# Attention by couples of heads or maps: fp32 scores on 64-row tiles, A's values on 64-column tiles, nothing split

## The chip, the cores and the metric

The kernel runs on one core of one Trainium2 chip. The metric is the device time of one execution in microseconds, the median over several runs. The core has five engines with queues of their own: TensorE (PE), VectorE (DVE), ScalarE (ACT), GpSimd (POOL) and SyncE (SP), which here issues all DMAs. A queue runs in order; an engine whose next instruction waits does nothing else.

## The reference

One encoder layer, applied to two request groups (prompt, sample) of 1024 tokens and 1024 channels with the same weights. A normalised and modulated input `h` is projected once; two attention branches read it, and their gated outputs are projected, merged and added to the input.

```python
mod = einsum('bd,de->be', silu(c), w_ada) + b_ada;  shift, scale, gate = split(mod, 3)
h = rms_norm(x, norm_g) * (1 + scale) + shift
qa, ka, va, za, qb, kb, vb, zb, ga, gb = split(h @ w_in)
# A: 8 query heads, 2 key/value heads, head size 64; RMSNorm and axial rotation of q and k
oa = softmax(qa @ ka.T / 8) @ va * silu(za)
# B: 4 heads, two softmax maps of size 64 per head, values of 128
pd = softmax(q0 @ k0.T / 8) - lam * softmax(q1 @ k1.T / 8)
ob = rms_norm(pd @ vb, subln_g) * (1 - lam_init) * silu(zb)
merged = sigmoid(ga) * (oa @ w_proj_a) + sigmoid(gb) * (ob @ w_proj_b)
return x + gate * (merged @ w_out)
```

## The kernel before

All data is fp32. Where precision is needed at the speed of single-pass products (type `fp32r`), an operand is split into a rounded part and the rest, and the products of the parts are added up in PSUM. The kernel does this for the weights and `h` (three products for one), for the queries and keys of all scores, and for A's values. Only B's values are plain fp32 products (`WHOLE`, L810).

For each group the program runs a head (keys and values of A, the first half of A's queries), then six phases of attention, then the projections. A phase weaves three streams: attention steps (`attention`), the projections for the next phase (`qa_gen`, `qkb_gen`, `vb_gen`, products at L497) and the gate paths (`z_gen`, products at L679). The weaving by shares (`ATT_W` and the like) and a priority for attention steps set where instructions stand; a scheduler puts them in each engine's order when the program is built, and nothing is moved at run time.

- `pairs_T` turns queries and keys by a PE transpose (L548). Each head's 64 rows are then written twice over 128 partitions: rounded on one half (L550, ACT), the rest on the other (L551, DVE). `swapped` makes a second copy of a piece of 256 queries with the halves exchanged, by two or four DMAs (tile `sw`).
- `scores` handles one head or map and one query tile of 128: four products over 128 partitions (L709 with the tile `q`, L710 with `sw`) fill one of two score tiles `s` in PSUM, 128 x 1024. DVE takes the maximum (L711), ACT the exponential with its sum (L712), which frees the tile.
- `flip` combines B's two maps (L744), transposes in blocks of 32 x 32 (L745, DVE) and regroups by four DMAs into a tile `q`, two query tiles making a unit of 256.
- `a_values`: for each of four pieces the turned probabilities are split (L758, ACT; L759, DVE), and 16 products of 256 columns (L770, L771) go into the one accumulator `a`. Since the values are split too, rows 0-63 and 64-127 of `a` are two parts of one head, added at L786 and L787.
- `b_values`: eight fp32 products of 256 columns (L810), no split.

A unit is one head (A) or one head of two maps (B) with 256 queries: per group 32 units in A and 16 in B. PSUM has two tiles `s`, three banks `f` for the projections and one bank `a`.

Of the kernel before, what the change touches and what calls it, by code (L numbers as in the profile page):

```python
# [64 lines left out]
BEHIND = 1.4  # L65
AHEAD = 100
PV_LAG = 2

WHOLE = (True, True)
# [21 lines left out]
def kernel(ctx: ExitStack, tc: tile.TileContext, t: dict):  # L91
# [8 lines left out]
    qpool = ent(tc.tile_pool(name="qpool", bufs=2))  # L100
    tpool = ent(tc.tile_pool(name="tpool", bufs=2))
# [403 lines left out]
    def rms(ps, nh, e):  # L505
# [3 lines left out]
        nc.scalar.activation(raw, ps, AF.Copy)  # L509
# [31 lines left out]
    def pairs_T(x3, even, odd):  # L541


        nb = x3.shape[1] // 2
        ps = gbank()[:, : nb * P].rearrange("p (b n) -> p b n", b=nb)
        x = x3.rearrange("p (b two) d -> p b (two d)", two=2)
        for b in range(nb):
            nc.tensor.transpose(ps[:, b, :], x[:, b, :], ident)  # L548
        for dst, hi, lo in ((even, LO, HI), (odd, HI, LO)):
            nc.scalar.activation(dst[hi], ps[hi], AF.Copy)  # L550
            nc.vector.tensor_tensor(out=dst[lo], in0=ps[hi], in1=dst[hi].bitcast(F32), op=ALU.subtract)  # L551
# [15 lines left out]
    def swapped(u):  # L567

        qs = u["q"]
        sw = mtile("sw", [P, 2, 256], F32R)[:, : len(qs)]  # L570
        sl = slice(u["pr"] * 256, u["pr"] * 256 + 256)
        for m, q in enumerate(qs):
            for a, b in ((LO, HI), (HI, LO)):
                dma(sw[a, m].bitcast(F32), q[b, sl].bitcast(F32))
        return sw


    made = {}

# [3 lines left out]
    def kva_gen(ht, out):  # L583
        w = kva_w.pop()[0] if kva_w else load_w(w_cols(w_in, (C_KA, 256)))
        k = v2(utile())
        va = utile().rearrange("p (n k d) -> p n k d", n=NTT, k=2)
        out["ka"], out["va"] = k, va

        def front(tt, ps):
            e = by_turns(tt)  # L590
            x3, s3 = rms(ps[:, :128], 2, e)
            vp = ps[:, 128:256].rearrange("p (k d) -> p k d", k=2)
            vt = va[:, tt]
            nc.scalar.activation(vt[:, :, 0:64], vp, AF.Copy)
            nc.vector.tensor_tensor(out=vt[:, :, 64:128], in0=vp, in1=vt[:, :, 0:64].bitcast(F32), op=ALU.subtract)
            e.tensor_tensor(out=x3, in0=x3, in1=gka.unsqueeze(1).to_broadcast([P, 2, HD]), op=ALU.mult)
            rope(x3, s3, out["cosA"][:, tt], out["sinA"][:, tt], 16, e)
            return x3

        def back(tt, x3):  # L600
            sl = slice(tt * P, (tt + 1) * P)
            pairs_T(x3, k[:, 0:1, sl], k[:, 1:2, sl])
# [3 lines left out]
    def qa_gen(st, half):  # L606
        w = load_w(w_cols(w_in, (C_QA + half * 256, 256)))
        qs = [v2(utile()), v2(utile())]
# [3 lines left out]
        def front(tt, ps):  # L612
            e = by_turns(tt)
            x3, s3 = rms(ps, 4, e)
# [4 lines left out]
        def back(tt, x3):  # L619
            sl = slice(tt * P, (tt + 1) * P)  # L620
            pairs_T(x3, qs[0][:, :, sl], qs[1][:, :, sl])
            made[id(qs)] = tt + 1
# [3 lines left out]
    def qkb_gen(ht, out, h):  # L626
        w = load_w(w_cols(w_in, (C_QB + h * P, P), (C_KB + h * P, P)))
        qk = out[h] = (v2(utile()), v2(utile()))
# [9 lines left out]
        def back(tt, x3):  # L638
            sl = slice(tt * P, (tt + 1) * P)
            pairs_T(x3, qk[0][:, :, sl], qk[1][:, :, sl])  # L640
            made[id(qk)] = tt + 1
# [3 lines left out]
    def vb_gen(ht, out, pr):  # L645
        w = load_w(w_cols(w_in, (C_VB + pr * 256, 256)))
        if WHOLE[pr]:
            v = utile().bitcast(F32).rearrange("p (n h e) -> p n h e", n=NTT, h=2)
            out[2 * pr], out[2 * pr + 1] = v[:, :, 0], v[:, :, 1]
        else:  # L650
            vs = [utile().rearrange("p (n s e) -> p n s e", n=NTT, s=2) for _ in range(2)]
            out[2 * pr], out[2 * pr + 1] = vs
        for tt in range(NTT):
            ps = yield from proj_tt(ht, w, tt)
            if WHOLE[pr]:
                nc.scalar.activation(v[:, tt].rearrange("p h e -> p (h e)"), ps, AF.Copy)
                yield 1
                continue
            for i in range(2):
                vp = ps[:, i * P : (i + 1) * P]  # L660
                nc.scalar.activation(vs[i][:, tt, 0, :], vp, AF.Copy)
                nc.vector.tensor_tensor(
                    out=vs[i][:, tt, 1, :], in0=vp, in1=vs[i][:, tt, 0, :].bitcast(F32), op=ALU.subtract
                )
# [38 lines left out]
    def softmax_unit(q, sw, k, pt, su):  # L703

        m = tiny.tile([P, 1], F32, tag="m", name=nm("m"))
        s = sbank()
        for n in range(2):
            sl = slice(n * 512, (n + 1) * 512)
            nc.tensor.matmul(s[:, sl], q, k[:, sl], start=True, stop=False)  # L709
            nc.tensor.matmul(s[:, sl], sw, k[:, sl], start=False, stop=True)  # L710
        nc.vector.tensor_reduce(out=m, in_=s, axis=AX.X, op=ALU.max, negate=True)  # L711
        nc.scalar.activation(  # L712
            pt.rearrange("p (j c a) -> p j c a", j=4, c=8), s.rearrange("p (c a j) -> p j c a", c=8, j=4),
            AF.Exp, bias=m, accum_out=su,
        )

    def scores(u, i):

        nm_ = len(u["q"])
        t, m = i // nm_, i % nm_  # L720
        qt = u["pr"] * 2 + t
        if "sw" not in u:
            u["sw"] = swapped(u)
        pt = ptile()
        su = u["su"][:, qt : qt + 1] if m == 0 else tiny.tile([P, 1], F32, tag="su", name=nm("su"))
        softmax_unit(u["q"][m][:, qt * P : (qt + 1) * P], u["sw"][:, m, t * P : (t + 1) * P], u["k"][m], pt, su)
        if m == 0:
            u[t] = [pt]
        else:
            f = tiny.tile([P, 1], F32, tag="r", name=nm("r"))  # L730
            nc.vector.reciprocal(f, su)
            nc.gpsimd.tensor_scalar(
                out=f, in0=f, scalar1=u["su"][:, qt : qt + 1], scalar2=nlam, op0=ALU.mult, op1=ALU.mult
            )
            u[t] += [pt, f]
        return t if m == nm_ - 1 else None

    def flip(u, t):


        pt = u[t][0]
        if len(u[t]) > 1:
            _, p1, f = u[t]
            nc.vector.scalar_tensor_tensor(out=pt, in0=p1, scalar=f, in1=pt, op0=ALU.mult, op1=ALU.add)  # L744
        nc.vector.transpose(pt, pt)  # L745
        if t == 0:
            u["pT"] = pair(F32R)
        dst = u["pT"].bitcast(F32).rearrange("p (i t f) -> p i t f", i=4, t=2)
        for i in range(4):
            dma(dst[:, i, t], pt[i * 32 : i * 32 + 32])  # L750

    def pT_pieces(u):

        pT = u["pT"].rearrange("p (q c b) -> p c q b", q=8, c=8)
        for cc in range(4):
            tl = pT[:, cc * 2 : cc * 2 + 2]
            th = tpool.tile([P, 2, 8, 32], F32R, tag="hi", name=nm("hi"), bufs=3)
            nc.scalar.activation(th, tl.bitcast(F32), AF.Copy)  # L758
            nc.vector.tensor_tensor(out=tl, in0=tl.bitcast(F32), in1=th.bitcast(F32), op=ALU.subtract)  # L759
            yield cc, th, tl  # L760

    def a_values(u):
        acc = ps_a.tile([P, 512], F32, tag="a", name=nm("a"))[:, :256]
        ready = []

        def pv(cc, th, tl):
            for c in range(2):
                k = cc * 2 + c
                lt = u["v"](k)
                nc.tensor.matmul(acc, lt, th[:, c, :], start=(k == 0), stop=False)  # L770
                nc.tensor.matmul(acc, lt, tl[:, c, :], start=False, stop=(k == 7))  # L771

        for piece in pT_pieces(u):
            ready.append(piece)
            if len(ready) > PV_LAG:
                pv(*ready.pop(0))
            yield 1
        while len(ready) > 1:
            pv(*ready.pop(0))
            yield 1  # L780
        pv(*ready.pop())
        tmp = mtile("at", [P, 256], bufs=1)
        o = mtile("oo", [P, 256])
        j = u["j"]
        a, b = (slice(0, 64), slice(64, 128)) if j % 2 == 0 else (slice(64, 128), slice(0, 64))
        nc.scalar.activation(tmp[a], acc[b], AF.Copy)  # L786
        nc.vector.tensor_tensor(  # L787
            out=query_order(o[a]), in0=piece_order(acc[a]), in1=piece_order(tmp[a]), op=ALU.add
        )
        pr = u["pr"]  # L790
        dma(u["od"][pr // 2][a, (pr % 2) * 256 : (pr % 2 + 1) * 256], o[a])
        yield 1

    def b_values(u):
        acc = ps_a.tile([P, 512], F32, tag="a", name=nm("a"))[:, :256]
        ready = []
        def pv(cc, th, tl):
            for c in range(2):
                k = cc * 2 + c
                for s, rt in ((0, th), (0, tl), (1, th)):  # L800
                    nc.tensor.matmul(
                        acc, u["v"][:, k, s, :], rt[:, c, :],
                        start=(k == 0 and s == 0 and rt is th), stop=(k == 7 and s == 1),
                    )

        if WHOLE[u["h"] // 2]:
            pT = u["pT"].bitcast(F32).rearrange("p (q c b) -> p c q b", q=8, c=8)
            yield 1
            for k in range(NCH):
                nc.tensor.matmul(acc, u["v"][:, k], pT[:, k], start=(k == 0), stop=(k == 7))  # L810
                if k % 2:
                    yield 1
        else:
            for piece in pT_pieces(u):
                ready.append(piece)
                if len(ready) > PV_LAG:
# [365 lines left out]
```

## Time and profile before

| | |
|---|---|
| median of 3 runs | 1984.13 us (1981.57 to 1989.72) |
| span of the profiled execution, the only time that the page gives of it | 1985.5 us |
| PE busy / weight loads busy | 1908.6 us / 1627.8 us |
| DVE, ACT, POOL busy | 1330.8, 1009.9, 758.1 us |
| mean granted TensorE clock | 0.982 |
| records of products, each with a weight load | 10466 |

The page gives busy times per engine, the span in 40 slices, the chain of work that ended last, and groups of instructions by source line. A row of a group reads: line, engine, operation, tile written <- tiles read, shape, count | busy us, mean ns of one | idle time of the engine just before them and what ended it. PEld are PE's weight loads, which have rows of their own. In a timeline a row is start, length (both us), engine, line, operation and count. An fp32 product leaves two records, an `fp32r` product one. Records of products overlap at their ends, so their rate is read from the starts.

### The profile page before, as it was taken

The page shows a single profiled execution, that of the slowest core. Times are in us where ns is not written, and L with a number is a line of the kernel's source. Part 1 is how long each engine was busy: PE and PEld are TensorE (multiplying, and loading weights), DVE is VectorE, ACT ScalarE, POOL GpSimd, SP SyncE. Part 2 cuts the span into 40 slices and gives each one's busy share as a digit, 9 for nine tenths or more (in the row PEclk, how much of TensorE's full clock was granted, in tenths as well). Part 3 has the DMA queues.
Part 4 walks back from the last instruction along what each step waited for, and adds up shares of the span by engine and source line. Part 5 has one row for each costly group of instructions (what it writes and reads, how often), then busy time and mean ns, then how long its engine had stood idle before and what let it go on. Part 6 is the DMA issues. An engine that isn't in the chain of part 4 may idle for free.

```text
span 1985.5 us, 30670 instructions
## 1 busy us (share of the span) xinstructions
PE 1908.6 (96%) x10466; PEld 1627.8 (82%) x10466; DVE 1330.8 (67%) x1906; ACT 1009.9 (51%) x1939; POOL 758.1 (38%) x1008
## 2 busy tenths in 40 slices
PE   8889999999999998999999899999999999999999
PEld 3878888888878994778888787888887888877887
DVE  4558877777877577547465877677788845665641
ACT  4435655665654444754323565556655534566310
POOL 2374612453446252221235464134445626422110
PEclk9899999999999999999999999999999999999999
DMA  8124556555553345865641455565654333567532
GB/s 310 33 80 126 155 152 169 152 166 154 133 153 102 101 120 173 257 227 167 222 149 35 140 144 145 149 164 144 184 137 137 106 97 99 156 212 245 174 101 75
DMA packets 269531, 295.11 MB, mean 149 GB/s; under 512 B 35776, under 2 KB 218176, under 8 KB 269376
## 3 DMA queue, kind: packets, MB, share of 16 engines
q1 hardware_dynamic: 269376, 293.15, 49.7%
q8 instruction: 84, 1.38, 0.3%
q14 instruction: 71, 0.58, 0.1%
HBM read 133.59 MB, written 42.01 MB: 88 GB/s over the span
## 4 chain that ended last, share of the span: by engine, by line
PE 68%; DMA 8%; DVE 8%; ACT 5%; SPq 4%; issue 3%; POOL 3%; ACTq 0%; POOLq 0%; DVEq 0%
PE f L497 16%; PE f L679 16%; PE f L950 6%; PE f L979 5%; PE s L709 4%; PE a L810 4%; PE s L710 4%; PE s L979 4%; DMA q<-p 3%; SPq L750 3%; PE s L950 2%; DVE q L759 2%; PE a L771 2%; PE a L770 2%; DVE m L711 2%
## 5 line engine op out<-in xcount | busy, mean ns | idle before, releaser
L679 PE MATMUL f<-u,w 128*128 128x512 f32 x2232 | 582.3, 398 | 0.1
L497 PE MATMUL f<-w,u 128*128 128x256 f32 x3456 | 487.0, 286 | 2.2 <-ACT ev L685 1.4
L497 PEld LDWEIGHTS f<-w,u 128*128 128x128 f32 x3456 | 459.5, 192 | 22.4 <-ACT ev L685 1.8
L679 PEld LDWEIGHTS f<-u,w 128*128 128x128 f32 x2232 | 408.8, 190 | 77.3 <-POOL w L181 0.8
L181 POOL TENSOR_TENSOR w<-st,w 128x512 fp32r<-128x512 f32 x168 | 230.3, 1390 | 439.9 <-ACT w L179 375.1
L712 ACT ACTIVATE p<-s,m 128x1024 f32<-128x1024 f32 x256 | 284.4, 1111 | 206.3 <-DVE m L711 111.3
L711 DVE TENSOR_REDUCE m<-s 128x1 f32<-128x1024 f32 x256 | 310.0, 1216 | 51.3 <-PE s L710 48.7
L745 DVE STREAM_TRANSPOSE p<-p 128x1024 f32<-128x1024 f32 x192 | 238.2, 1241 | 99.2 <-ACT p L712 86.5
L759 DVE TENSOR_TENSOR q<-q,hi 128x512 fp32r<-128x512 f32 x256 | 198.3, 792 | 60.6 <-ACT hi L758 58.6
L515 POOL TENSOR_TENSOR rs<-ss,nhalf 128x4 f32<-128x4 f32 (+1 forms) x112 | 112.8, 1007 | 322.8 <-DVE ss L514 284.0
L758 ACT ACTIVATE hi<-q 128x512 fp32r<-128x512 f32 x256 | 153.8, 625 | 104.1 <-DMA q<-p 55.4
L710 PE MATMUL s<-u,sw 128*128 128x512 f32 x512 | 206.7, 404 | 0.0
L179 ACT ACTIVATE w<-st 128x512 fp32r<-128x512 f32 x196 | 113.9, 625 | 97.2 <-DMA st<-in_w_in_dram 46.0
L950 PE MATMUL f<-u,w 128*128 128x512 f32 x552 | 133.4, 395 | 5.1 <-ACT ev L685 4.4
L770 PE MATMUL a<-hi,u 128*128 128x256 f32 x512 | 132.5, 285 | 2.1 <-DVE oo L787 2.1
L771 PE MATMUL a<-q,u 128*128 128x256 f32 x512 | 129.8, 286 | 1.2 <-DVE q L759 1.2
L810 PE MATMUL a<-q,u 128*128 128x256 f32 x512 | 128.3, 390 | 1.9 <-DVE oo L826 1.5
L950 PEld LDWEIGHTS f<-u,w 128*128 128x128 f32 x552 | 103.9, 190 | 27.2 <-ACT ev L685 4.7
L709 PE MATMUL s<-u 128*128 128x512 f32 x256 | 110.9, 433 | 15.1 <-ACT p L712 15.1
L810 PEld LDWEIGHTS a<-q,u 128*128 128x128 f32 x512 | 97.8, 196 | 17.5 <-DVE oo L826 1.6
L709 PE MATMUL s<-u,u 128*128 128x512 f32 x256 | 103.6, 405 | 8.3 <-ACT p L712 7.7
L710 PEld LDWEIGHTS s<-u,sw 128*128 128x128 f32 x512 | 98.4, 192 | 15.5
(175 smaller groups left out, 2562.1 us busy)
## 6 DMA issues: line engine op xcount, KB each, us to landing
q<-p SPq DMA_DIRECT2D x768, 128.0 KB, 2.6
st<-in_w_in_dram SPq DMA_DIRECT2D x132, 256.0 KB, 3.0
zd<-ev SPq DMA_DIRECT2D x96, 256.0 KB, 2.2
sw<-u SPq DMA_DIRECT2D x256, 64.0 KB, 2.1
p<-zd SPq DMA_DIRECT2D x64, 256.0 KB, 3.2
u<-in_w_ada_dram SPq DMA_DIRECT2D x8, 1024.0 KB, 10.4
st<-in_w_in_dram SPq DMA_DIRECT2D x64, 128.0 KB, 2.7
st<-in_w_out_dram SPq DMA_DIRECT2D x32, 256.0 KB, 2.9
```

The source lines that it names most:

```text
L181: e.tensor_tensor(out=wl, in0=st, in1=wh.bitcast(F32), op=ALU.subtract)
L497: nc.tensor.matmul(ps, lt[c][:, sl], w[:, c, wi, :], start=(k == 0), stop=(k == 23))
L679: nc.tensor.matmul(ps, w[:, c, wi, e * P : (e + 1) * P], rt[c], start=(k == 0), stop=(k == 23),)
L709: nc.tensor.matmul(s[:, sl], q, k[:, sl], start=True, stop=False)
L710: nc.tensor.matmul(s[:, sl], sw, k[:, sl], start=False, stop=True)
L711: nc.vector.tensor_reduce(out=m, in_=s, axis=AX.X, op=ALU.max, negate=True)
L712: nc.scalar.activation(pt.rearrange("p (j c a) -> p j c a", j=4, c=8), s.rearrange("p (c a j) -> p j c a", c=8, j=4), AF.Exp, bias=m, accu ...
L745: nc.vector.transpose(pt, pt)
L759: nc.vector.tensor_tensor(out=tl, in0=tl.bitcast(F32), in1=th.bitcast(F32), op=ALU.subtract)
L810: nc.tensor.matmul(acc, u["v"][:, k], pT[:, k], start=(k == 0), stop=(k == 7))
L950: nc.tensor.matmul(ps, w[:, c, wi, d * P : (d + 1) * P], o[:, oi, :], start=(k == 0), stop=(k == 11))
L979: nc.tensor.matmul(ps, w[:, c, wi, e * P : (e + 1) * P], m[:, mi, :], start=(k == 0), stop=(k == 23))
```

## The change

Two heads of A that share a place in their key/value groups (j and j + 4), or the two maps of a B head, form a couple. One transpose puts the first in partitions 0-63 and the second in 64-127, and one ACT copy writes them, unsplit, in fp32 (`turned` in place of `pairs_T`). The columns of A's query weights are loaded in an order that makes such couples. `swapped` and its DMAs are gone, and so are the splits of the probabilities and of A's values.

`scores` now handles a couple and a query tile: four fp32 products of 512 columns, alternating between partitions 64-127 and 0-63, into both tiles `s` at once. Each contracts over 64 partitions and so uses a tile of 64 rows of the array. `a_values` makes 16 fp32 products of 256 columns, alternating between two column halves of the array: the first head's values end in rows 0-63 of `a`, the second's in 64-127, and one ACT copy takes both out. Nothing is added up. `together` binds the products of one group so that nothing stands between them; the first score product of a couple also waits for both exponentials of the couple before. A has 16 units per group (couples with 256 queries), B 16 as before. The pool of regrouped tiles grows from two to three, the pool of split pieces goes. The steps and their shares in the weaving are rewritten for the new count (`PAIRS`).

```diff
+PAIRS = (1.3, 0.3)
+TOP = 100000
-PV_LAG = 2
-WHOLE = (True, True)
...
-    qpool = ent(tc.tile_pool(name="qpool", bufs=2))
-    tpool = ent(tc.tile_pool(name="tpool", bufs=2))
+    qpool = ent(tc.tile_pool(name="qpool", bufs=3))
...
-        for dst, hi, lo in ((even, LO, HI), (odd, HI, LO)):
-            nc.scalar.activation(dst[hi], ps[hi], AF.Copy)
-            nc.vector.tensor_tensor(out=dst[lo], in0=ps[hi], in1=dst[hi].bitcast(F32), op=ALU.subtract)
+        nc.scalar.activation(to, ps, AF.Copy)
+
+    def behind(ins, other, kind):
+        tc.add_manual_dep(ins.ins, other.ins.name, mybir.DependencyInfo(kind, mybir.DependencyReason.DATA))
+
+    def together(calls, after=()):
+        prev = None
+        for call in calls:
+            if prev is None:
+                ins = call()
+                for other in after:
+                    behind(ins, other, mybir.DependencyClass.Sync)
+            else:
+                with tc.high_priority(offset=TOP):
+                    ins = call()
+                behind(ins, prev, mybir.DependencyClass.NoSync)
+            prev = ins
...
-        w = load_w(w_cols(w_in, (C_QA + half * 256, 256)))
-        qs = [v2(utile()), v2(utile())]
+        w = load_w(w_cols(w_in, (C_QA + half * P, P), (C_QA + 256 + half * P, P)))
+        qs = v2(utile().bitcast(F32))
...
-            nc.tensor.matmul(s[:, sl], q, k[:, sl], start=True, stop=False)
-            nc.tensor.matmul(s[:, sl], sw, k[:, sl], start=False, stop=True)
...
+    def scores(u, t):
+        qt = u["pr"] * 2 + t
+        ss = [sbank(), sbank()]
+        qs = slice(qt * P, (qt + 1) * P)
+        calls = []
         for n in range(2):
             sl = slice(n * 512, (n + 1) * 512)
+            for m in (1, 0):
+                rows = (LO, HI)[m]
+                calls.append(lambda m=m, rows=rows, sl=sl: nc.tensor.matmul(
+                    ss[m][:, sl], u["q"][rows, qs], u["k"][rows, sl], start=True, stop=True
+                ))
+        together(calls, list(exps))
+        exps.clear()
...
-            nc.scalar.activation(th, tl.bitcast(F32), AF.Copy)
-            nc.vector.tensor_tensor(out=tl, in0=tl.bitcast(F32), in1=th.bitcast(F32), op=ALU.subtract)
...
     def a_values(u):
         acc = ps_a.tile([P, 512], F32, tag="a", name=nm("a"))[:, :256]
+        pT = [x.rearrange("p (q c b) -> p c q b", q=8, c=8) for x in u["pT"]]
+        together([
+            lambda k=k, m=m: nc.tensor.matmul(
+                acc[(LO, HI)[m]], u["v"][:, k, m], pT[m][:, k], start=(k == 0), stop=(k == 7)
+            )
+            for k in range(NCH) for m in (1, 0)
+        ])
+        yield 1
+        o = mtile("oo", [P, 256])
+        nc.scalar.activation(query_order(o), piece_order(acc), AF.Copy)
```

What this does to the engines' orders is seen at three places. Line numbers of the changed kernel are its own: there L712 is a score product, L750 one of A's values, L667 and L495 are the gate and projection products (L679 and L497 before), L694 the maximum, L741 the block transpose.

PE, a score tile of A in the first group before (`s`; `sw` the swapped queries, `f` the projections' banks, `w` weights, `u` long-lived tiles):

```order
L497 MATMUL f_5494<-w_5391,u_327 128x256
L709 MATMUL s_5294<-u_396,u_1453 128x512
L710 MATMUL s_5294<-u_396,sw_5162 128x512
L709 MATMUL s_5294<-u_396,u_1453 128x512
L710 MATMUL s_5294<-u_396,sw_5162 128x512
L497 MATMUL f_5494<-w_5391,u_327 128x256
L497 MATMUL f_5494<-w_5391,u_328 128x256
```

and a couple at a like place of the changed kernel:

```order
L667 MATMUL f_3910<-u_547,w_3705 128x512
L712 MATMUL s_4085<-u_393,u_1399 128x512
L712 MATMUL s_4084<-u_393,u_1399 128x512
L712 MATMUL s_4085<-u_393,u_1399 128x512
L712 MATMUL s_4084<-u_393,u_1399 128x512
L667 MATMUL f_3910<-u_547,w_3705 128x512
L667 MATMUL f_3910<-u_548,w_3705 128x512
```

One tile `s` was filled with four products over all rows; now two are filled in turns by four products over half the rows, which stand without anything between them.

PE, part of A's values before (`hi` and `q` the two parts of the turned probabilities):

```order
L770 MATMUL a_5079<-hi_5101,u_397 128x256
L771 MATMUL a_5079<-q_4916,u_397 128x256
L770 MATMUL a_5079<-hi_5119,u_397 128x256
L771 MATMUL a_5079<-q_4916,u_397 128x256
L770 MATMUL a_5079<-hi_5119,u_397 128x256
L771 MATMUL a_5079<-q_4916,u_397 128x256
L497 MATMUL f_5577<-w_5391,u_283 128x256 x2
L497 MATMUL f_5577<-w_5391,u_284 128x256
L497 MATMUL f_5577<-w_5391,u_283 128x256 x2
L709 MATMUL s_5325<-u_396,u_1453 128x512
L710 MATMUL s_5325<-u_396,sw_5266 128x512
L709 MATMUL s_5325<-u_396,u_1453 128x512
```

and the beginning of a group of values after:

```order
L667 MATMUL f_3993<-u_529,w_3705 128x512 x2
L667 MATMUL f_3993<-u_530,w_3705 128x512
L750 MATMUL a_4137<-q_3972,u_393 64x256
L750 MATMUL a_4137<-q_3971,u_393 64x256
L750 MATMUL a_4137<-q_3972,u_393 64x256
L750 MATMUL a_4137<-q_3971,u_393 64x256
```

The products were written at full height and could stand apart, with a score tile among them; now they write 64 rows each, from two tiles `q`, and stand in one block of 16.

DVE in A's first phase before (`m` maximum, `p` probabilities, `ss` sums for RMSNorm, `oo` output):

```order
L711 TENSOR_REDUCE m_3954<-s_3955 128x1
L514 TENSOR_SCALAR ss_4295<-ss_4295 128x4
L551 TENSOR_TENSOR u_3851<-f_4307,u_3851 64x2x128
L745 STREAM_TRANSPOSE p_3869<-p_3869 128x1024
L759 TENSOR_TENSOR q_3425<-q_3425,hi_3691 128x2x8x32
L759 TENSOR_TENSOR q_3591<-q_3591,hi_3767 128x2x8x32
L711 TENSOR_REDUCE m_4041<-s_4042 128x1
L759 TENSOR_TENSOR q_3591<-q_3591,hi_3804 128x2x8x32
L745 STREAM_TRANSPOSE p_3953<-p_3953 128x1024
L759 TENSOR_TENSOR q_3591<-q_3591,hi_3812 128x2x8x32
L787 TENSOR_TENSOR oo_3752<-a_3625,at_3751 64x4x2x32
L711 TENSOR_REDUCE m_4145<-s_4146 128x1
```

and after:

```order
L694 TENSOR_REDUCE m_1983<-s_1975 128x1
L694 TENSOR_REDUCE m_1986<-s_1976 128x1
L741 STREAM_TRANSPOSE p_1981<-p_1981 128x1024
L741 STREAM_TRANSPOSE p_1982<-p_1982 128x1024
L516 TENSOR_REDUCE ss_2151<-row_2148 128x4
L517 TENSOR_SCALAR ss_2151<-ss_2151 128x4
L694 TENSOR_REDUCE m_2016<-s_2008 128x1
L694 TENSOR_REDUCE m_2019<-s_2009 128x1
L741 STREAM_TRANSPOSE p_2014<-p_2014 128x1024
L741 STREAM_TRANSPOSE p_2015<-p_2015 128x1024
```

Splits (L551, L759) and adding (L787) are gone; two maxima follow each other, and the two block transposes of a couple stand behind them.

More of the change, by code (lines that the diff above doesn't have):

```diff
@@ L717, in scores @@
[L717 to L728, printed above, removed]
-        else:
+            for m in (1, 0):
+                rows = (LO, HI)[m]
+                calls.append(lambda m=m, rows=rows, sl=sl: nc.tensor.matmul(
+                    ss[m][:, sl], u["q"][rows, qs], u["k"][rows, sl], start=True, stop=True
+                ))
@@ L752, in pT_pieces @@
[L752 to L760, printed above, removed]
+            nc.vector.reciprocal(f, sus[1])
+            nc.gpsimd.tensor_scalar(out=f, in0=f, scalar1=sus[0], scalar2=nlam, op0=ALU.mult, op1=ALU.mult)
@@ new lines, in scores @@
+            u[t] = pts, f
+        else:
+            u[t] = pts, None
+    def flip(u, t):
+        pts, f = u[t]
+        if f is not None:
+            nc.vector.scalar_tensor_tensor(out=pts[0], in0=pts[1], scalar=f, in1=pts[0], op0=ALU.mult, op1=ALU.add)
+            pts = pts[:1]
+        if t == 0:
+            u["pT"] = [pair() for _ in pts]
+        for pt, pT in zip(pts, u["pT"]):
+            nc.vector.transpose(pt, pt)
+            dst = pT.rearrange("p (i t f) -> p i t f", i=4, t=2)
+            for i in range(4):
+                dma(dst[:, i, t], pt[i * 32 : i * 32 + 32])
@@ L872, in attention @@
                 late = []
-                if t is not None:
-                    late.append(lambda u=live[n], t=t: flip(u, t))
-                    if t == (0 if ph < 2 else 0) and n + 1 < len(units) and units[n + 1][2]():
-                        live[n + 1] = units[n + 1][1]()
-                        late.append(lambda u=live[n + 1]: u.update(sw=swapped(u)))
+                if qk:
+                    late.append(lambda u=live[n], t=i: flip(u, t))
             yield None
@@ L1033, in b_unit @@
             }
-        def there(kind, n, pr):
-            return made.get(id(st[kind].get(n)), 0) > 2 * pr + 1
         units = []
```

183 lines of the change are left out of this document (55 added, 128 removed).

## The prediction

> **What bounds the kernel now.** I read the page first: busy shares, slices, the chain.
>
> ```profile
> span 1985.5 us, 30670 instructions
> ...
> PE 1908.6 (96%) x10466; PEld 1627.8 (82%) x10466; DVE 1330.8 (67%) x1906; ACT 1009.9 (51%) x1939; POOL 758.1 (38%) x1008
> ...
> PE   8889999999999998999999899999999999999999
> ...
> PE 68%; DMA 8%; DVE 8%; ACT 5%; SPq 4%; issue 3%; POOL 3%; ACTq 0%; POOLq 0%; DVEq 0%
> ```
>
> TensorE is busy in nearly every slice; no other engine is above 67%. So the sum has to be made on PE: what the change adds to its stream is paid in full, and what it takes from the others pays only where PE waits for them. The waits of PE's weight loads (PEld), the long ones on what the change touches:
>
> ```profile
> PEld s L709 <- ACT p L712: 32.5, 25, 4.2
> PEld f L548 <- ACT u L550: 6.7, 3, 2.9
> PEld f L950 <- ACT ev L685: 4.7, 1, 4.7
> PEld f L832 <- ACT ev L685: 4.1, 1, 4.1
> ```
>
> Columns: us in total, times, longest. The scores lose 32.5 us waiting for an exponential to free their PSUM tile. All four together, 48 us, are what lighter engines could give back at most.
>
> Next, the rate of each kind of product, from the timeline of PE. A product's duration holds its latency; the rate is the distance between starts.
>
> ```profile
> 1301.61 0.39 PE L709 MATMUL s<-u,u 128*128 128x512 f32 x1
> 1301.84 0.39 PE L710 MATMUL s<-u,sw 128*128 128x512 f32 x1
> 1302.07 0.39 PE L709 MATMUL s<-u,u 128*128 128x512 f32 x1
> 1302.29 0.39 PE L710 MATMUL s<-u,sw 128*128 128x512 f32 x1
> 1302.52 0.28 PE L770 MATMUL a<-hi,u 128*128 128x256 f32 x1
> ...
> 1307.08 0.28 PE L770 MATMUL a<-hi,u 128*128 128x256 f32 x1
> ...
> 1308.40 0.28 PE L771 MATMUL a<-q,u 128*128 128x256 f32 x1
> 1308.51 0.29 PE L497 MATMUL f<-w,u 128*128 128x256 f32 x1
> ```
>
> A split score product of 512 columns takes 0.23 us of PE; a head's tile has four. From 1307.08 to 1308.51 stand twelve split value products of 256 columns: 0.119 each. The price of an fp32 product shows in branch B's values and in the products of the ada weights:
>
> ```profile
> 1507.83 3.61 PE L810 MATMUL a<-q,u 128*128 128x256 f32 x16
> 1511.29 0.38 PE L548 MATMUL f<-ident,row 128*128 128x128 f32 x2
> ...
> 761.19 0.39 PE L710 MATMUL s<-u,sw 128*128 128x512 f32 x1
> 761.51 1.88 PE L435 MATMUL f<-st,cT 128*2 128x512 f32 x4
> 763.32 0.50 PE L709 MATMUL s<-u 128*128 128x512 f32 x1
> 763.66 0.39 PE L710 MATMUL s<-u,sw 128*128 128x512 f32 x1
> ...
> L435 PE MATMUL f<-st,cT x32: 591/592/1061, 752.6 to 786.2; 128*2 128x512 f32 x32
> ```
>
> Eight fp32 products of L810 are 16 records; 3.46 us to the next start, so 0.215 per record, 0.43 per product of 256 columns. For 512 columns a record takes 0.429: four records and the rest of the last one, whose median is 0.592 (the row of the source line), make 1.88, so (1.88 - 0.592) / 3. Each fp32 product is two such records on the same tile, one after the other.
>
> **PE, scores.** A couple (two heads of A, or two maps of B) for one query tile was 8 split products, 8 x 0.23 = 1.84 us. It becomes four fp32 products of 512 columns, two on rows 0-63 and two on rows 64-127: eight records of 0.429. Nothing in this trace runs two tiles of the array beside each other, so the cost is bounded by cases: 8 x 0.429 = 3.43 if one after the other, 4 x 0.429 = 1.72 if fully side by side. I take a case between: records start in program order, and that order is upper tile, upper, lower, lower, upper, upper, lower, lower. The second upper record waits for the first, so the lower tile starts one slot late and the group takes five slots, 2.15 us. I choose it since every fp32 run above keeps its two records in order and nothing here shows a record passing another. 2.15 - 1.84 = +0.305; 128 couples (64 in A, 64 in B): **+39 us**.
>
> The Trainium skill, "TensorE: Matmul & The Clock Gate", section "The mechanism", says that products on different row groups run concurrently, but that products keep program order at start and end, only weight loads being pulled ahead. By it the group takes the five slots; no run here shows it yet.
>
> **PE, A's values.** A couple took 32 split products, 32 x 0.119 = 3.81 us. Now 16 fp32 products, 32 records of 0.215 alternating in pairs between column halves: 17 slots, 3.66 us, if they run beside each other as above; 6.88 if not, 3.44 if fully. -0.15 x 32 couple-units (4 couples, 4 pieces, 2 groups): **-5 us**. B's values are the same fp32 products as before: 0.
>
> **PE, the change of tile.** Before, nearly every product used the whole array. Now 128 score groups and 32 value groups are each entered and left. Two rows price this. Above, L710 starts at 761.19, its successor was due 0.23 later at 761.42, and the 2-column product starts at 761.51: 0.09 lost. Its four records end at 763.23; L709 starts at 763.32 and is 0.50 long instead of 0.39, its weights not loaded ahead: 0.09 + 0.11 lost. The second price, a 2-row product:
>
> ```profile
> 787.52 0.39 PE L710 MATMUL s<-u,sw 128*128 128x512 f32 x1
> 787.84 0.41 PE L442 MATMUL f<-ident,row 2*128 2x2 f32 x4
> 788.18 0.50 PE L679 MATMUL f<-u,w 128*128 128x512 f32 x1
> ...
> 1730.75 1.08 PE L679 MATMUL f<-u,w 128*128 128x512 f32 x4
> 1731.67 0.27 PE L889 MATMUL f<-ident,suA 128*64 128x128 f32 x1
> 1731.69 1.61 PE L679 MATMUL f<-u,w 128*128 128x512 f32 x6
> ```
>
> Again 0.09 on entry (787.52 + 0.23 = 787.75), and 0.11 of weights on leaving (0.50 against 0.39). As seen, that is 0.09 + 0.20 = 0.29 per group; with 128-column weights not loaded ahead on entry either, 0.40, the upper end. The lower end is 0: the 64-column L889 sits at 1731.67, where a fifth L679 would have stood (1730.75 + 4 x 0.23), without a gap. I take 0.30, near the two that lose time, for a change of rows is what they show: 160 x 0.30 = **+48 us** (0 to 64).
>
> The Trainium skill, "TensorEngine Tiling (Array Packing)", section "Key Properties", says that changing the tiling mode drains TensorE. The 0.09 gaps agree with it, L889's row does not; by that row the 32 value groups would be free, 10 us less.
>
> **The other engines.**
>
> ```profile
> L711 DVE TENSOR_REDUCE m<-s 128x1 f32<-128x1024 f32 x256 | 310.0, 1216 | 51.3 <-PE s L710 48.7
> L712 ACT ACTIVATE p<-s,m 128x1024 f32<-128x1024 f32 x256 | 284.4, 1111 | 206.3 <-DVE m L711 111.3 <-DMA q<-p 84.4 <-DVE r L731 3.0
> L759 DVE TENSOR_TENSOR q<-q,hi 128x512 fp32r<-128x512 f32 x256 | 198.3, 792 | 60.6 <-ACT hi L758 58.6 <-DMA zd<-ev 1.0
> L758 ACT ACTIVATE hi<-q 128x512 fp32r<-128x512 f32 x256 | 153.8, 625 | 104.1 <-DMA q<-p 55.4 <-PE a L770 42.5 <-PE s L710 1.9
> L551 DVE TENSOR_TENSOR u<-f,u 64x256 fp32r<-64x256 f32 (+1 forms) x196 | 80.4, 411 | 35.1 <-ACT u L550 29.3
> L712 ACT ACTIVATION_READ_ACCUMULATOR p<-s,m 128x1 f32 x256 | 49.2, 192 | 0.0
> ...
> sw<-u SPq DMA_DIRECT2D x256, 64.0 KB, 2.1
> ...
> sum 1350.00, PE 1302.28 PEld 1127.65 DVE 982.74 ACT 764.76 POOL 557.63; mean PE 325.57 PEld 281.91 DVE 245.69 ACT 191.19 POOL 139.41
> ```
>
> Gone: the splits of the turned probabilities (L758 154 us of ACT, L759 198 of DVE), the splits after the transposes (L551, 80 of DVE; L550's two half-height copies become one), the adding of A's two halves (L786, L787), and 256 DMAs for the swapped queries on SP's queue. The 768 DMAs q<-p stay, and so do POOL's rows; the rearranged columns of A's q weights add 16 short DMAs. All of it lies beside PE's work, so none counts by itself. What counts is PE's wait for it: I take back 28 of the 32.5 us at L709, all 7 at L548 and the 9 at the two waits for ACT's L685, **-44 us** (0 to -48).
>
> New is that a couple needs both score tiles at once, and the first product waits for both exponentials. From a couple's last product: max 1.22, then exp 1.11 + 0.19 beside the second max, then the second exp 1.30: 3.8 us in which the next couple cannot start. Everything behind a waiting score product on PE's queue stands too. Fill covers it: the two groups' attention takes some 1350 us (last row, the sum of the stretches 150 to 450, 450 to 850, 1100 to 1400 and 1450 to 1800), 10.5 per couple, of which a couple itself needs 2.5, so 8 us of projection or value products stand against 3.8. The 4.5 us that I leave of the 32.5 are for places where it is thinner. If that cover were gone at each couple it would cost 128 x 3.8 = 486 us, the price of no forecast here.
>
> Sum: 39 - 5 + 48 - 44 = +38 on the profiled 1985.5, which stands 1.4 above the median: **2022 us**, 1.9% slower. With the bounds 39 - 5 + 0 - 48 to 39 - 5 + 64 - 0, that is 1970 to 2082 for this case alone.
>
> **Rivals.**
> - *Fully side by side* (the other side: faster). Each tile takes its own records as they come, so neither waits for the other's second. Scores 1.72: -0.12 x 128 = -16; values 3.44: -0.37 x 32 = -12; +48 - 44. Sum -24: **1960**, with the same bounds 1907 to 2019. For it: two halves of the array share no rows (scores) or no columns (values). Against: no row shows it. It decides from a score group of about 1.85 us including all but the change of tile.
> - *Scores overlap, values don't*: two column halves stream from the same 128 partitions. Values 6.88: +98 instead of -5; sum +141: **2125**. The Trainium skill, "TensorE: Matmul & The Clock Gate", section "The mechanism", says that weight loads overlap running products only where the row group differs, which speaks for this. Against: whole-array loads of the same rows overlap here already (PEld is 82% busy beside PE).
> - *Nothing overlaps* (the change doesn't do what its tiles are for): scores 3.43, +204; values +98; +48 - 44. Sum +306: **2290**. For it: fp32 is two records everywhere; against: nothing in the trace excludes overlap, since disjoint tiles never follow each other in it.
>
> **How the numbers follow.** Five slots 0.40, fully side by side 0.35, values serial 0.10, nothing overlaps 0.15. The range 1945 to 2130 takes the first three but for the lowest part of the second, and leaves out the last: some 0.2 outside. About 0.5%, 10 us, is what can be told from no change. The first case, 1970 to 2082 around 2022, is faster than 1974 in 0.12, within in 0.18; the second, around 1960, faster in 0.74, within 0.17. So faster 0.31, same 0.13, slower 0.56.
>
> **What would show it.** In the timeline of PE, a score group's eight records: starts in five slots of 0.43 (forecast), four (1960) or eight (2290); from the last product before a group to the first after it, 2.45 us. In a value group the distance from first to last start, some 3.5 or 6.7. L758, L759 and sw gone from the groups. The waits of the scores for the exponential under 10 us; if they grow to tens, the cover was thinner than 8 us and the forecast is too low. DVE's busy time should fall by some 280 us (198 + 80) with no gain in time from it: if the time falls by more than 25 us, PE waited on more than its idle rows show.

## The result and the profile after

The changed kernel takes 2047.61 us (median of four runs, 2046.52 to 2048.32), 3.2% more than before (ratio 1.0322, 95% interval 1.0299 to 1.0345). The profiled execution has a span of 2044.6 us, 59.1 above the 1985.5 of before. From its page, spans, busy times and the slices of PE:

```profile
span 2044.6 us, 29062 instructions
...
PE 1935.9 (95%) x10466; PEld 1471.7 (72%) x10466; DVE 1022.0 (50%) x1346; ACT 810.3 (40%) x1539; POOL 707.6 (35%) x1008
...
PE   8989999999999997799999899999999999976999
```

DVE has lost 309 us and ACT 200, as the removal of the splits has it, and the time went up. Two places in PE's row are new: 77 in the middle and 76 near the end. They are the last attention phases of the two groups. Span less busy time gives PE's idle time: 108.7 us, against 76.9 before, 31.8 more.

The timeline of PE around a score group (L712 are its products, 8 records), then around a group of A's values (L750, 32 records):

```profile
405.68 1.29 PE L667 MATMUL f<-u,w 128*128 128x512 f32 x5
406.90 1.99 PE L712 MATMUL s<-u,u 64*128 64x512 f32 x8
408.82 0.98 PE L495 MATMUL f<-w,u 128*128 128x256 f32 x6
...
206.80 0.48 PE L667 MATMUL f<-u,w 128*128 128x512 f32 x1
207.21 3.67 PE L750 MATMUL a<-q,u 128*64 128x256 f32 x32
210.81 0.70 PE L712 MATMUL s<-u,u 64*128 64x512 f32 x2
```

Eight records of 0.429 would take 3.43 us in a row and 2.15 in five slots. L712 takes 1.99, and that includes 0.10 for its first weights and 0.16 by which the last record outlasts its slot: 1.72, four slots. The two tiles run fully side by side. The same holds for L750: 3.67 less 0.05 and 0.16 is 3.46, sixteen slots of 0.216. A cut of the same timeline, from 406.95 to 407.3, shows two records in one slot:

```profile
406.90 0.70 PE L712 MATMUL s<-u,u 64*128 64x512 f32 x2
```

Around the score group nothing is hidden: five L667 at 0.228 from 405.68 end their slots at 406.82, and L712 starts at 406.90; its last slot ends at 408.72 (406.90 + 0.10 + 1.72), L495 starts at 408.82. The loads of weights, in the row of PEld, say the same:

```profile
406.90 0.30 PEld L712 LDWEIGHTS s<-u,u 64*128 64x128 f32 x4 [0.35 <-issue]
...
408.82 0.89 PEld L495 LDWEIGHTS f<-w,u 128*128 128x128 f32 x7 [0.76 <-ACT w L177]
```

The first weights of a group are loaded when it starts and not ahead, likewise the first ones behind it. Each side costs some 0.09 of gap and 0.10 of weights, 0.39 us per score group. The first record of L712 is 0.70 long instead of 0.59, which is the 0.10 again. For a value group it is 0.34, since its 64-column weights cost 0.05 on entry (its first record is 0.43 long, the others 0.38).

PE's waits, us in total, times, longest:

```profile
PE a L769 <- DMA q<-p: 30.2, 5, 15.5
PE s L712 <- ACT p L695: 17.1, 7, 7.1
PE s L895 <- ACT w L220: 9.8, 1, 9.8
PE a L769 <- DVE oo L775: 7.5, 3, 3.6
```

L769, the unchanged values of B, waits 30 us for its turned probabilities. Its row on the page, and the row of the same products before:

```profile
L769 PE MATMUL a<-q,u 128*128 128x256 f32 x512 | 138.6, 416 | 46.7 <-DMA q<-p 30.2
L810 PE MATMUL a<-q,u 128*128 128x256 f32 x512 | 128.3, 390 | 1.9 <-DVE oo L826 1.5
```

PE now stands idle 46.7 us before these products and not 1.9; the rise is larger than that of PE's whole idle time, so other waits have shrunk. The products themselves are busy 10.3 us longer. The chain to the longest of these waits, in the second group's last phase, by the timelines of PE, ACT, DVE and SP, and the row of its window 1862 to 1868 (us, busy time of PE, PEld, DVE, ACT and POOL with counts, granted clock, DMA share, GB/s):

```profile
1845.85 0.60 PE L860 MATMUL s<-ident,ssB 128*128 128x128 f32 x4
1862.00 5.29 PE L769 MATMUL a<-q,u 128*128 128x256 f32 x16 [15.54 <-DMA q<-p]
...
1841.74 1.11 ACT L695 ACTIVATE p<-s,m 128x1024 f32<-128x1024 f32 x1
...
1842.95 1.28 ACT L850 ACT_TABLE_LOAD   x1
1846.32 0.63 ACT L850 ACTIVATE q<-q 128x512 f32<-128x512 f32 x1 [2.08 <-DMA q<-zd]
1846.97 1.28 ACT L695 ACT_TABLE_LOAD   x1
1848.26 1.11 ACT L695 ACTIVATE p<-s,m 128x1024 f32<-128x1024 f32 x1
...
1849.50 0.16 DVE L726 RECIPROCAL r<-su 128x1 f32<-128x1 f32 x1 [1.76 <-ACT p L695]
1851.44 0.75 DVE L861 SCALAR_TENSOR_TENSOR q<-q,subg 128x512 f32<-128x512 f32 x1 [1.78 <-ACT q L850]
1852.11 1.28 DVE L736 SCALAR_TENSOR_TENSOR p<-p,r,p 128x1024 f32<-128x1024 f32 x1
...
1855.32 0.69 DVE L906 TENSOR_TENSOR u<-f,p 128x512 f32<-128x512 f32 x1 [0.67 <-ACT p L886]
1855.92 1.23 DVE L741 STREAM_TRANSPOSE p<-p 128x1024 f32<-128x1024 f32 x1
...
1857.19 2.50 SPq L744 DMA_DIRECT2D q<-p x4
...
1862.00:1868.00 6.00, 5.29 (x16) 4.07 (x16) 0.75 (x1) 5.03 (x5) 0.00 (x0) 0.73 0.81 276
```

Other steps stand in this chain on two engines. On ACT the second exponential of the couple runs 5.4 us behind the end of the first: between them stand a SiLU of the gating (L850), its wait for a loaded tile and two table loads. On DVE a gating step that waits for that SiLU (L861) stands ahead of the combining L736, and a second one with a merging step of the projections (L906) ahead of the transpose L741, some 4.5 us in all. So the four DMAs leave only at 1857.19. PE has nothing else in its row and stands for 15.5 us. The wait costs more than its length: behind it the granted clock is 0.73, and the 16 records take 5.29 us where B's values took 3.61 before.

So there are two questions: is the change of tile really what the score groups cost, and why did the lighter engines return nothing?

### The profile page after: what moved, and what is told of

The parts are those of the page before. It is cut to its first block, busy times and chain, and to the rows that moved or that the text cites. A ratio compares the mean times of both kernels' runs of the same rounds, so it can differ in the third digit from the quotient of the medians.

```text
span 2044.6 us, 29062 instructions
## 1 busy us (share of the span) xinstructions
PE 1935.9 (95%) x10466; PEld 1471.7 (72%) x10466; DVE 1022.0 (50%) x1346; ACT 810.3 (40%) x1539; POOL 707.6 (35%) x1008
## 5 line engine op out<-in xcount | busy, mean ns | idle before, releaser
L667 PE MATMUL f<-u,w 128*128 128x512 f32 x2232 | 573.8, 400 | 0.5 <-ACT u L551 0.2
L667 PEld LDWEIGHTS f<-u,w 128*128 128x128 f32 x2232 | 404.9, 190 | 117.7 <-issue 36.8
L495 PEld LDWEIGHTS f<-w,u 128*128 128x128 f32 x3456 | 446.1, 191 | 59.3 <-issue 39.5
L495 PE MATMUL f<-w,u 128*128 128x256 f32 x3456 | 477.2, 287 | 1.8 <-ACT ev L673 1.8
L694 DVE TENSOR_REDUCE m<-s 128x1 f32<-128x1024 f32 x256 | 301.2, 1218 | 342.6 <-PE s L712 342.4
L741 DVE STREAM_TRANSPOSE p<-p 128x1024 f32<-128x1024 f32 x192 | 234.0, 1235 | 47.7 <-ACT p L695 41.6
L769 PE MATMUL a<-q,u 128*128 128x256 f32 x512 | 138.6, 416 | 46.7 <-DMA q<-p 30.2
L769 PEld LDWEIGHTS a<-q,u 128*128 128x128 f32 x512 | 102.8, 211 | 71.0 <-issue 41.9
L712 PE MATMUL s<-u 64*128 64x512 f32 x512 | 130.1, 624 | 10.3 <-ACT p L695 10.1
L712 PE MATMUL s<-u,u 64*128 64x512 f32 x512 | 131.2, 623 | 7.1 <-ACT p L695 7.1
L895 PE MATMUL f<-u,w 128*128 128x512 f32 x552 | 132.3, 395 | 0.0
L516 DVE TENSOR_REDUCE ss<-row 128x4 f32<-128x256 f32 (+1 forms) x112 | 44.0, 393 | 164.9 <-ACT row L513 152.5
L750 PE MATMUL a<-q,u 128*64 128x256 f32 x1024 | 118.4, 382 | 1.2 <-issue 0.7
L895 PEld LDWEIGHTS f<-u,w 128*128 128x128 f32 x552 | 103.9, 190 | 21.4
L727 POOL TENSOR_SCALAR r<-r,suB,nlam 128x1 f32<-128x1 f32 x64 | 22.2, 347 | 272.4 <-DVE r L726 272.3
L924 PE MATMUL f<-u,w 128*128 128x512 f32 x456 | 105.6, 389 | 0.0
L736 DVE SCALAR_TENSOR_TENSOR p<-p,r,p 128x1024 f32<-128x1024 f32 x64 | 86.6, 1354 | 34.3 <-POOL r L727 29.8
L750 PEld LDWEIGHTS a<-q,u 128*64 128x64 f32 x1024 | 73.2, 137 | 39.8 <-issue 6.5
```

What stands on the lines that cost most here:

```text
L495: nc.tensor.matmul(ps, lt[c][:, sl], w[:, c, wi, :], start=(k == 0), stop=(k == 23))
L667: nc.tensor.matmul(ps, w[:, c, wi, e * P : (e + 1) * P], rt[c], start=(k == 0), stop=(k == 23),)
L712: calls.append(lambda m=m, rows=rows, sl=sl: nc.tensor.matmul(ss[m][:, sl], u["q"][rows, qs], u["k"][rows, sl], start=True, stop=True))
L750: lambda k=k, m=m: nc.tensor.matmul(acc[(LO, HI)[m]], u["v"][:, k, m], pT[m][:, k], start=(k == 0), stop=(k == 7))
L895: nc.tensor.matmul(ps, w[:, c, wi, d * P : (d + 1) * P], o[:, oi, :], start=(k == 0), stop=(k == 11))
L924: nc.tensor.matmul(ps, w[:, c, wi, e * P : (e + 1) * P], m[:, mi, :], start=(k == 0), stop=(k == 23))
```

## Experiments

Ratios are to the kernel before on the same chip, with their 95% intervals. Four runs were made on a second chip, where the kernel before takes 1978.16 us and not 1984: the one without the splits, the one with both kinds of pacing, the unbound one and the one without the added wait. Where they are compared with the changed kernel, it is by the ratio.

**Do the tiles depend on each other's order?** In the changed kernel:

```diff
-        for n in range(2):
...
-            for m in (1, 0):
...
+        for m in (1, 0):
...
+            for n in range(2):
```

> The four products of a score group in another order: both of the upper rows, then both of the lower. Theory 1, each tile of the array takes its own records as they come, far ahead of the other's: the group still takes four slots of 0.43 us, the time stays at 2048 us (ratio to before 1.03). Theory 2, records start in program order and a record that waits for its tile holds up those behind it: the lower tile could start only with the last upper record, seven slots, +1.29 us x 128 = +165 us, 2213 us (1.115).

Measured: 2051.47 us, ratio 1.0344 (1.0326 to 1.0362). The interval overlaps that of the changed kernel. From the timeline of PE, the group, and a cut of it from 408.45 to 408.8:

```profile
408.36 1.99 PE L712 MATMUL s<-u,u 64*128 64x512 f32 x8
...
408.36 0.71 PE L712 MATMUL s<-u,u 64*128 64x512 f32 x2
```

The program has four records of the upper tile first, and still the lower tile's first record starts 13 ns behind the upper's, and the group takes the same 1.99 us. A record that waits for its tile does not hold up the other tile's. Theory 1 stands. The rule of the Trainium skill ("TensorE: Matmul & The Clock Gate", section "The mechanism") that products keep program order at their start does not hold here across tiles.

**What does a change of tile cost?** A one-column product over the whole array stands in the middle of each score group:

```diff
+        calls.insert(2, lambda: nc.tensor.matmul(ss[0][:, 512:513], ident, ones_c, start=True, stop=True))
         together(calls, list(exps))
```

> A product of one column over the whole array (128 weights, its result is overwritten) is put into the middle of each score group, so that each group is left and entered once more. Theory, leaving and entering costs 0.39 us as the gaps of the changed kernel show (0.09 + 0.10 on either side): with the product's own two records of 0.11 it is +0.61 x 128 = +78 us, 2126 us (ratio 1.071). Rival, the gaps belong to waits at the groups' ends and not to the change of tile: only the product itself, +28 us, 2076 us (1.046).

Measured: 2101.62 us, ratio 1.0598 (1.058 to 1.0616), 54 us over the changed kernel: between the two forecasts. The timeline of PE says why:

```profile
417.55 1.13 PE L712 MATMUL s<-u,u 64*128 64x512 f32 x4
418.61 0.38 PE L715 MATMUL s<-ones_c,ident 128*128 128x1 f32 x2
418.92 1.13 PE L712 MATMUL s<-u,u 64*128 64x512 f32 x4
```

The first four records end their slots at 418.51; without the product the second half would run on from there, now it starts at 418.92 and has its 0.10 of weights again: 0.51 us for exit, product and entry together. 128 x 0.51 = 65 us is also what PE's busy time grew by (2000.6 against 1935.9 us); PE's waits for L769's probabilities, for the exponentials and for the weights of L895 fell by 11 in all:

```profile
PE a L770 <- DMA q<-p: 26.3, 6, 10.5
PE s L712 <- ACT p L695: 13.0, 5, 6.8
...
PE s L896 <- ACT w L220: 7.1, 1, 7.1
```

(L770 and L896 are L769 and L895, one line on.) The cost stands in PE's stream at each group and not at waits, so the rival, 28 us, falls. How the 0.51 divides was not measured: with 0.39 for the change of tile, 0.12 are left for the product; with the 0.22 that I gave the product, 0.29 are left for the change.

**One part alone: A's values.** The kernel before, with split scores, but with unsplit values of two neighbouring heads on 64-column tiles (steps, their shares and the pools are adapted too):

```diff
+    def a_values(first, u):
...
+        pT = [x["pT"].rearrange("p (q c b) -> p c q b", q=8, c=8) for x in (first, u)]
+        together([
+            lambda k=k, m=m: nc.tensor.matmul(
+                acc[(LO, HI)[m]], u["v"](k), pT[m][:, k], start=(k == 0), stop=(k == 7)
+            )
+            for k in range(NCH) for m in (1, 0)
+        ])
...
-                for i in (0, 2, 1, 3) for pr in range(4)
+                for c in range(2) for pr in range(4) for i in (2 * c, 2 * c + 1)
```

> The kernel before with one part of the change alone: A's values unsplit on 64-column tiles, two neighbouring heads of a key/value group as a couple; scores stay split products over the whole array. Theory, the loss lies in the scores (128 groups that change tiles, and couples that need both score tiles at once): PE is nearly even here (16 slots of 0.215 + 0.34 against 3.81 us per couple), DVE and ACT lose the splits, time 1975 to 1985 us (ratio 0.995 to 1.0). Rival 1, the relief of DVE and ACT is worth what the forecast took: 1955 to 1965 us (0.985 to 0.99). Rival 2, unsplit values on column tiles are themselves the loss (change of tile, values that wait for all their pieces): 2000 us or more (1.008).

Measured: 1973.86 us, ratio 0.9952 (0.9933 to 0.9971); once more with more rounds:

> The kernel with A's values alone on column tiles (e_values) once more, in more rounds: 1974 us, ratio 0.993 to 0.997, if its gain stands; rival, it was chance and the ratio is 0.998 to 1.002.

Measured: 1977.74 us, ratio 0.997 (0.9955 to 0.9984). So it is faster than the kernel before, by some 0.3%, and than the changed one. In this second run DVE has 219 us less to do than before and ACT 147, and the waits of the scores (L721 here) are nearly what they were, 32.5 us before:

```profile
PE 1897.3 (96%) x10466; PEld 1572.7 (80%) x10466; DVE 1112.1 (56%) x1570; ACT 862.9 (44%) x1653; POOL 722.4 (37%) x1008
...
PEld s L721 <- ACT p L724: 27.4, 15, 5.2
```

The values are therefore not where the 59 us lie; the scores and what follows from them are.

**What is the relief alone worth?** The kernel before, its products reading the unsplit pieces:

```diff
...
-            nc.scalar.activation(th, tl.bitcast(F32), AF.Copy)
-            nc.vector.tensor_tensor(out=tl, in0=tl.bitcast(F32), in1=th.bitcast(F32), op=ALU.subtract)
-            yield cc, th, tl
+            yield cc, tl, tl
```

> The kernel before without the splits of A's turned probabilities (L758 and L759, 154 us of ACT and 198 us of DVE): both products read the unsplit piece, so A's values are no longer exact; PE's stream is unchanged. Theory, PE's waits before were latency of chains and not load of DVE and ACT, so the relief that the change brings is worth 0 to 14 us: 1970 to 1984 us (ratio 0.993 to 1.0). Rival, the forecast's term: the waits of the scores go with the load, 28 to 44 us: 1940 to 1956 us (0.978 to 0.986).

Measured: 1976.71 us, ratio 0.9985 (0.9966 to 1.0004), no difference that can be told. From its page and its waits:

```profile
PE 1906.9 (96%) x10466; PEld 1631.3 (82%) x10466; DVE 1144.7 (58%) x1650; ACT 876.8 (44%) x1687; POOL 723.2 (37%) x1008
...
PEld s L709 <- ACT p L712: 23.3, 13, 4.6
```

DVE has 186 us less to do and ACT 133, and the scores still wait 23 of 32.5 us. The rival, 28 us or more, falls. The 23 us do not come from these two splits; that they are the length of the chain product, maximum, exponential at places with little fill is argued and not shown, since L551's splits and the copies of the queries are still there.

**Does the tail come from gating?** The changed kernel with `GATED_A = -0.6` for -0.2:

> The changed kernel with the gating steps of the last attention phase woven in later (GATED_A -0.6 for -0.2). Theory, the long waits of B's last values (5 to 15 us each) come from gating steps, which wait for their loads on DVE and stand ahead of the transposes: later gating gives back 25 to 35 us, some 2018 us (ratio 1.017). Rival, PE waits there since the other work has run out: no gain, or up to 10 us more, 2048 to 2058 us (1.032 to 1.037).

Measured: 2024.8 us, ratio 1.0207 (1.019 to 1.0224): 23 us given back, a little less than the theory had. PE's idle time falls by 21 us, to 87.5. L769's wait for the probabilities falls from 30.2 to 6.0; a part of the gain moves to the projections (L895), which now wait for the gating:

```profile
PE a L769 <- DMA q<-p: 6.0, 3, 2.9
...
PE f L895 <- ACT u L866: 6.1, 2, 3.9
```

The same with the values of B further behind their scores as well:

```diff
-GATED_A = -0.2
+GATED_A = -0.4
...
-BEHIND = 1.4
+BEHIND = 1.9
```

> The changed kernel with both kinds of pacing: gating of the last phase somewhat later (GATED_A -0.4) and B's values half a unit further behind their scores (BEHIND 1.9 for 1.4). Theory, what is left of the loss is PE's own: scores -16, values -12, changes of tile 160 x 0.39 = +62, so 1985 + 34 = 2019 us and not below 2010 whatever the pacing (ratio 1.013 to 1.018). Rival, the couples' waits are all that is wrong and pacing can take the time to that of before, under 1995 us (1.005).

Measured: 2018.79 us, ratio 1.0213 (1.0188 to 1.0237). That the time falls on the theory's 2019 is in part chance: on this chip it is 41 us over the kernel before, the ratio lies above the theory's 1.013 to 1.018, and PE's own terms give 34 (-16 - 11 + 61). PE is still idle for 87.3 us, 10 more than before, and 34 + 10 comes near the 41. By the ratio pacing returns 1.1%, some 22 us, no more than the later gating of -0.6 alone (1.0207), so what the second setting adds cannot be told. The rival, under 1995 us, falls: pacing does not reach the time before.

The later gating does nothing where the scores are split (e_values with `GATED_A = -0.4`):

> The kernel with A's values alone on column tiles, with the gating of the last phase later (GATED_A -0.4 for -0.2). Theory, B's last values wait some 8 us for their transposed probabilities behind gating steps, as in the changed kernel: 1964 to 1972 us (ratio 0.990 to 0.994). Rival, with the split scores the attention ends early enough, and later gating only moves the wait to the projections: 1974 to 1982 us (0.995 to 0.999).

Measured: 1978.51 us, ratio 0.998 (0.9967 to 0.9993); the rival holds.

**What the binding is worth.** The changed kernel with `together` reduced to its first product's wait:

```diff
-                with tc.high_priority(offset=TOP):
-                    ins = call()
-                behind(ins, prev, mybir.DependencyClass.NoSync)
+                ins = call()
```

> The changed kernel with the products of a group not bound to each other. The scheduler then leaves 93 of the 128 score groups whole and breaks up the others; the value groups stay whole. Theory, every break costs a change of tile (0.39 us) and a product that has lost its partner another 0.86 us: some 60 breaks and 70 single products, +40 to +70 us, 2088 to 2118 us (ratio 1.052 to 1.067). Rival, other work between the products fills waits, so that it costs nothing: 2048 us (1.032).

Measured: 2134.8 us, ratio 1.0791 (1.0769 to 1.0814), by the ratios some 93 us over the changed kernel and more than I had counted; the direction is the theory's. The loss is in PE's stream and not in waits: PE is busy for 2025.7 us, 90 more than in the changed kernel, and idle for 6 less. In the trace some 93 score groups stand whole, as expected, but only 24 of the 32 value groups do; 68 score products and 48 value products stand alone. The binding itself sets the order and a priority and does not wholly keep other work out: in the changed kernel's trace 122 of the 128 score groups stand whole and six are cut in two.

And the opposite piece, bound products without the added wait (`together(calls)` for `together(calls, list(exps))`):

> The changed kernel without the added wait of a couple's first product for both exponentials; the waits for the two score tiles themselves stay. Theory, the tile waits come to the same, since a group cannot end before the second tile is free: 2043 to 2050 us (ratio 1.030 to 1.033). Rival, the added wait is what costs the 17 us that the scores wait for the exponentials: 2030 us (1.023).

Measured: 2090.27 us, ratio 1.0569 (1.0549 to 1.059), by the ratios some 49 us slower than the changed kernel. Neither theory had this. From its timeline of PE, score products only:

```profile
529.60 1.99 PE L712 MATMUL s<-u 64*128 64x512 f32 x8
537.10 1.12 PE L712 MATMUL s<-u 64*128 64x512 f32 x2
539.68 1.98 PE L712 MATMUL s<-u 64*128 64x512 f32 x6
```

At 529.60 a group is whole. At 537.10 one product runs alone (two records, 0.10 + 0.86 + 0.16), 2.58 us before the other three, which take the full four slots. The first product was placed where its own tile `s` came free, with other work behind it: its partner is lost and the array changes tile once more. In the whole trace only some 55 of the 128 groups stand whole. PE's idle time does fall without the added wait, by 34 us to 75.0, but its busy time grows by 76, to 2011.7. The wait for both exponentials pays for itself, since it keeps the couple together.

## Why the prediction was right or wrong

The direction held, and 2047.6 lies between 1945 and 2130. The forecast of 2022 was 26 too low, with three terms off that partly cancel. That it came near, and even the direction, is in part luck: with the four slots of the trace in place of the five, and the other terms as forecast, the same sum would have given 1967, faster than before. The kernel is slower because of the change of tile and of new waits, not because of the scores' slots.

| term | forecast | measured | from |
|---|---|---|---|
| scores in slots | +39 (five) | -16 (four, (1.716 - 1.84) x 128) | timeline after, e_blocked |
| A's values in slots | -5 (17) | -11 (16, (3.46 - 3.81) x 32) | timeline after |
| change of tile | +48 (0.30 x 160) | +61 (0.39 x 128 + 0.34 x 32) | timeline after, e_switch |
| PE's waits | -44 | +25 (59 - 34, the rest) | waits after, e_gates, e_nosplit |

- *Five slots* failed: "the lower tile starts one slot late". It starts with the upper one. The rival "fully side by side" had this step right. Its time of 1960 fell, and so did its turning point (a score group of 1.85 us): the groups took 1.72 and the kernel was slower.
- *The change of tile* was mis-sized: the weights of both sides are exposed, which is the upper end of the range for score groups. (Sixteen value groups run straight into a score group, so the trace has 314 entries and exits where this sum counts 320.) The 64-column groups pay too, unlike L889's row; here the rule of the Trainium skill ("TensorEngine Tiling (Array Packing)", section "Key Properties") that a change of mode drains the array agrees, and the single transpose of before was a poor stand-in.
- *The relief* failed: "I take back 28 of the 32.5 us at L709, all 7 at L548 and the 9". Taking the splits of the probabilities away by themselves returned nothing measurable. By the row that the forecast used, the scores' waits did fall, from 32.5 to 21.3 us, 11 of the 28. But new waits came before B's values in the last phases, 46.7 us in place of 1.9, and with them slower products behind; the place of the gating accounts for 23 us (e_gates).
- *The couple's wait* was covered on the whole: the scores wait 17 us and not 486. The forecast had named tens there as the sign of being too low, and 17 us by PE's row, 21 by PEld's, is that sign.
- *B's values, cost 0*, held for the number of their records and not for their wait for `q<-p`, nor for the clock behind it.

What stays open: the 25 us are a remainder; PE's idle time, read directly, grew by 31.8, and what makes up the difference was not taken apart. Later gating returns 23 us, but which part of that is ACT's row and which DVE's was not tested, nor what holds the 10 us of idle time that pacing leaves.

## What to carry to other kernels

On a saturated TensorE, small tiles that run side by side need a group long enough to pay for its entry and exit: here a group of 1.72 us saved 0.12 and paid 0.39, while a group of 3.46 saved 0.35 and paid 0.34. Work taken off an engine that PE does not wait for by its load was worth nothing measurable here, so ask of each wait whether it would be shorter with the engine idle. When instructions are to overlap as a pair, let the first wait for what the last needs, or a scheduler may place it alone.

## What the runs showed of the hardware that was not expected

- Two 64-row or 64-column tiles overlap fully even when fp32 gives each several records in a row, for the 64-row tiles in either program order (1.99 us for the group in both). Their weight loads overlap too, also for column tiles that read the same partitions (16 slots of 0.216).
- Entering and leaving such a group costs a gap of 0.09 us and the unhidden first weights on each side, 0.39 us for 128 weight columns and 0.34 for 64. With a one-column product between two such groups, exit, product and entry took 0.51.
- Behind a wait of PE of 15.5 us the granted clock was 0.73 and B's values took 5.29 us, against 3.61 without such a wait.
